# A hybrid encoder layer: the first group's feature-major products computed as seven quarter products in their own stage, and token norms multiplied into the rows

## The chip, the cores and the metric

One core of one Trainium2 chip. The metric is device time in microseconds, median of the runs shown. The profile is one further execution on the same kind of core.

## What is computed

One layer of a bidirectional encoder, on two groups of tokens with shared weights: a sample of 1024 rows and a prompt of 256 rows, each of 2048 features. The kernel treats the 1280 rows as two halves of 640 ("first group" and "second group"). Cut to what matters:

```python
hn = rms_norm(x, norm_g)                       # per row: x / rms(x) * g
proj = hn @ w_in                               # 2048 x 4896
xbc, z_ssd, dt_raw, q, k, v, z_att, mq, z_mem = split_cols(proj, IN_SIZES)
xbc = silu(centred_dwconv(xbc, conv_w, conv_b))     # 5 taps along the tokens, 1536 channels
o_ssd = rms_norm((ssd_fwd + ssd_bwd + d_skip * xs) * silu(z_ssd), ssd_norm_g)
o_att = window_attention(rms_norm(q), rms_norm(k), v, sink) * silu(z_att)
mk, mv = split_cols(rms_norm(mem) @ w_mem_kv, (512, 512))   # 256 memory rows for each request
o_mem = softmax(rms_norm(mq) @ rms_norm(mk)) @ mv * silu(z_mem)
y = x + concat([o_ssd, o_att, o_mem]) @ w_out
```

## The kernel before

**Precision.** Every large product is made of three matmuls of split numbers: an operand is rounded to a high part H, and the rest is a low part L; the products HH, HL and LH are added up in PSUM. `wsplit` (L213) makes the split of a weight tile: a copy on ScalarE (ACT, L215) and a subtraction on VectorE (DVE, L216). The activations are split once for each group into eight tiles `xH0..3`, `xL0..3` (16 feature tiles of 128 by 640 rows) by `fill_direct` (L197): load, then ACT with the gain of the feature, then DVE. The norm of a row is not in there: `x_stats` (L1181) computes 1/rms of each row, tile by tile, and the evictions multiply it in.

**Blocks.** The work of TensorE (PE) is a sequence of blocks, written out at L1316 to L1402. `block_tok` (L239) gives row-major results: for 16 feature tiles k, five row tiles, three matmuls of 512 columns each, 240 in all (192 with the four tiles of the memory rows; 288 columns in the block "kv"). Weights come as tiles of 256 KB from the SP queue, four buffers `wraw`, three each for `wh` and `wl`. `block_feat` (L273) gives feature-major results for 256 output features: 16 k, two halves of features, two halves of rows (320 columns), three matmuls: 192. The convolution's six blocks ("x") and the gates of attention ("za") and memory ("zm"), two each, are made this way, because their results are used with features on partitions; `ev_conv` (L349) multiplies by the norms (`rbc`, a row vector of norms on all partitions, built by the matmuls `prx` in `x_rows`, L1229) and applies the five taps on DVE; `ev_gateT` (L318) makes the gate.

**Order.** mk and mv (memory keys and values), then for the first group q, kv, za, x, mq, zm, z0, z1, for the second kv, x, q, za, z0, z1, mq, zm, then the output: four blocks for the first group, and for the second group eight units of `block_pair` (L1147). That is a 2 x 2 block product by seven quarter products in place of eight (a Strassen scheme): for each unit of two times 128 output features, eight k, seven products, three matmuls of 320 columns: 168. `weight_sums` (L1132) makes the sums of weight quarters on GpSimd (POOL), `seven_sums` and the functions after it (L1052) the sums of row quarters, ahead of time; evictions (`ev_pair`, L1097) add the seven products up.

**Lanes.** All else (statistics, preparation of keys, attention, the scan) is cut into small steps, in two queues called lanes. After each k of a block `pump` (L171) takes steps by the rate in `RATES` or `MR` (steps for each k of lane 0 and lane 1). `need` (L182) runs a lane until something is done. A scheduler places the instructions within each engine's in-order stream: weight splits are drawn ahead by a priority offset, and a lane's instruction is placed no earlier than the last split (`marks`). The lanes' tiles lie in the pools `cl` and `mp`, `w2` (L398) being a ring of five buffers. Statistics pieces (512 features of 128 rows, 256 KB) are loaded by SP into that ring and squared with a sum on ACT (L1187 and L1199). SP issues all loads and stores in order.

The first group's lanes begin with `mem_stats` in the second half of mk; `x_stats` of the first group follow in mv and q.

Of the kernel before, what the change touches and what calls it, by code (L numbers as in the profile page):

```python
# [19 lines left out]
P = 128  # L20
# [6 lines left out]
MR = ((1.0, 0), (1.25, 0))  # L27
# [15 lines left out]
def hymba_encoder_kernel(  # L43
# [3 lines left out]
    mq_norm_g, mk_norm_g, x_turned, mem_turned, w_in_laid, w_mem_laid, w_out_laid, w_out_pairs, vecs,  # L47
# [20 lines left out]
    beside = ExitStack()  # L68
    cl = beside.enter_context(tc.tile_pool(name="cl", bufs=1))
    mp = beside.enter_context(tc.tile_pool(name="mp", bufs=2))  # L70
# [10 lines left out]
    def psum(name):  # L81
# [8 lines left out]
    upper = lconst([P, P], "upper")  # L90
    G.affine_select(out=upper, in_=ones, compare_op=ALU.is_ge, fill=0.0, base=0,
                    pattern=[[1, P]], channel_multiplier=-1)
# [8 lines left out]
    kT = lconst([P, 2, 7 * P], "kT", F32R)  # L101
    kL = lconst([P, 2, 7 * P], "kL", F32R)
    v_all = lconst([P, 7, P], "v_all")
    dt_all = lconst([P, NT, 32], "dt_all")
    eacs_all = lconst([P, NT, 32], "eacs_all")
    cd_all = lconst([P, NT, 32], "cd_all")

    wj_all = lconst([P, 6, 32], "wj_all")
    dd_all = lconst([P, 6, 32], "dd_all")
    rx = const([P, 14], "rx")  # L110
    rxh = const([P, NT], "rxh")
    rbc = lconst([P, 640], "rbc")
    carry = lconst([P, 12, 4], "carry")
    state = lconst([P, 1024], "state")
    mkH = lconst([P, 4, 256], "mkH", F32R)
    mkL = lconst([P, 4, 256], "mkL", F32R)
    mv = lconst([P, 2, 512], "mv")

# [14 lines left out]
    mv_d = dram([P, 2, 512], "mv_d")  # L133
# [63 lines left out]
    def fill_direct(q, j, src, gain=None, n=640):  # L197

        ch = rp.tile([P, 640], F32, tag="ch", name="chd", bufs=CH)[:, :n]
        last_load[0] = S.dma_start(ch, src)  # L200
        yield
        if j == 0:
            new_quad(q)
        h, l = cur["H", q][:, j, :n], cur["L", q][:, j, :n]
        if gain is None:
            A.activation(h, ch, AF.Copy)
            V.tensor_sub(l, ch, h.bitcast(F32))
        else:
            A.activation(h, ch, AF.Copy, scale=gain)
            V.scalar_tensor_tensor(out=l, in0=ch, scalar=gain, in1=h.bitcast(F32), op0=ALU.mult, op1=ALU.subtract)  # L210
        yield
# [98 lines left out]
    def ev_gate(c, base):  # L310
        def f(i, ps):
            z = ev.tile([P, 512], F32, tag="evt" if i % 2 else "evu", name="zs")
            A.activation(z, ps, AF.Tanh, scale=rxh[:, base + i:base + i + 1])
# [4 lines left out]
    def ev_gateT(c, grp, f0):  # L318
        def f(fc, ps):
            th = ev.tile([P, 640], F32, tag="evt", name="th")  # L320
            z = ev.tile([P, 640], F32, tag="evu", name="zs")
            for b in range(2):
                s_ = slice(b * 320, b * 320 + 320)
                V.tensor_mul(z[:, s_], ps[b][:, :320], rbc[:, s_])
            A.activation(th, z, AF.Tanh, scale=0.5)
            V.scalar_tensor_tensor(out=z, in0=th, scalar=1.0, in1=z, op0=ALU.add, op1=ALU.mult)
# [10 lines left out]
    def ev_dtkv(base):  # L337
        def f(i, ps):
            t = base + i
            rt = rx[:, t:t + 1]  # L340
            r = ev.tile([P, P], F32, tag="evt" if i % 2 else "evu", name="kraw")
            A.activation(r, ps[:, 32:160], AF.Copy, scale=rt)
            S.dma_start(k_d[t], r)
            V.scalar_tensor_tensor(out=dt_all[:, t, :], in0=ps[:, :32], scalar=rt, in1=dtb, op0=ALU.mult, op1=ALU.add)
            V.tensor_scalar(out=v_all[:, i + (2 if base else 0), :], in0=ps[:, 160:288], scalar1=rt, scalar2=None,
                            op0=ALU.mult)
        return f

    def ev_conv(grp, f0):  # L349
        def f(fc, ps):  # L350
            fc = f0 + fc
            u = ev.tile([P, 650], F32, tag="evu", name="u")
            if grp == 0:
                n = 638
                V.memset(u[:, :2], 0.0)
                V.tensor_mul(u[:, 2:322], ps[0][:, :320], rbc[:, :320])
                V.tensor_mul(u[:, 322:642], ps[1][:, :320], rbc[:, 320:])
                V.tensor_copy(carry[:, fc, :], u[:, 638:642])
            else:
                n = 646  # L360
                V.tensor_copy(u[:, 0:4], carry[:, fc, :])
                V.memset(u[:, 388:392], 0.0)
                V.memset(u[:, 648:650], 0.0)
                V.tensor_mul(u[:, 4:324], ps[0][:, :320], rbc[:, :320])
                V.tensor_mul(u[:, 324:388], ps[1][:, :64], rbc[:, 320:384])
                V.tensor_mul(u[:, 392:648], ps[1][:, 64:320], rbc[:, 384:])
            cw = [vec[:, R_CW + k * 12 + fc:R_CW + k * 12 + fc + 1] for k in range(5)]
            c = ev.tile([P, 650], F32, tag="evt", name="c")
            V.tensor_scalar(out=c[:, :n], in0=u[:, :n], scalar1=cw[0], scalar2=vec[:, R_CB + fc:R_CB + fc + 1],
                            op0=ALU.mult, op1=ALU.add)  # L370
            for k in range(1, 5):
                V.scalar_tensor_tensor(out=c[:, :n], in0=u[:, k:k + n], scalar=cw[k], in1=c[:, :n],  # L372
                                       op0=ALU.mult, op1=ALU.add)
            th = ev.tile([P, 650], F32, tag="evt", name="tc")
            A.activation(th[:, :n], c[:, :n], AF.Tanh)
            V.scalar_tensor_tensor(out=th[:, :n], in0=th[:, :n], scalar=1.0, in1=c[:, :n],
# [3 lines left out]
            else:  # L380
                S.dma_start(xbc_d[fc, :, 638:1024], th[:, :386])
                S.dma_start(xbc_d[fc, :, 1024:1280], th[:, 390:646])
        return f
# [17 lines left out]
    def ev_mk(i, ps):  # L401
        kr = ev.tile([P, 512], F32, tag="evt" if i % 2 else "evu", name="mkr")
        A.activation(kr, ps, AF.Copy)
        S.dma_start(mq_d[i], kr)

    def ev_mv(i, ps):
        if i < 2:
            A.activation(mv[:, i, :], ps, AF.Copy, scale=rx[:, 10 + i:11 + i])
        else:
            o = ev.tile([P, 512], F32, tag="evu", name="mvo")  # L410
            A.activation(o, ps, AF.Copy, scale=rx[:, 10 + i:11 + i])
            S.dma_start(mv_d[:, i - 2, :], o)

    def mk_prep(i):
        kr = w2("mkr")
        S.dma_start(kr, mq_d[i])
# [26 lines left out]

    def mem_swap(_):

        S.dma_start(mv, mv_d)
# [116 lines left out]
    def attn(t):  # L563
# [12 lines left out]
        A.activation(sq, q, AF.Square, scale=rx[:, t:t + 1])  # L576
# [7 lines left out]
        V.scalar_tensor_tensor(out=q3, in0=q3, scalar=rx[:, t:t + 1], in1=hb(r, 8, 64), op0=ALU.mult, op1=ALU.mult)  # L584
# [99 lines left out]
    def mem_attn(t):  # L684
# [6 lines left out]
        A.activation(sq, q, AF.Square, scale=rx[:, t:t + 1])  # L691
# [6 lines left out]
        V.scalar_tensor_tensor(out=q3, in0=q3, scalar=rx[:, t:t + 1], in1=hb(r, 4, P), op0=ALU.mult, op1=ALU.mult)  # L698
# [81 lines left out]
    def ssd_up(t):  # L780
        first = t in (0, NS)
        last = t in (NS - 1, NT - 1)
        tok = slice(t * P, (t + 1) * P)
        bc = mp.tile([P, 4, P], F32, tag="bc", name="bc", bufs=1)
# [191 lines left out]
    def ssd_down(t):  # L976
# [25 lines left out]
        for g in range(2):  # L1002
# [9 lines left out]
            A.activation(z, y, AF.Square, scale=rxh[:, t:t + 1], accum_out=ss[:, g:g + 1])  # L1012
# [116 lines left out]

    ahead = []  # L1130

    def weight_sums(i):  # L1132

        if i == 64:
            return
# [336 lines left out]
```

## Time and profile before

| what | value |
|---|---|
| median of 3 runs | 1842.91 us (1841.83 to 1843.0) |
| the profiled execution | 1841.09 us, its span 1839.4 us |
| PE, weight loads, DVE, ACT, POOL busy | 1828.2, 1647.2, 1161.1, 825.1, 230.4 us |
| moved by DMA | 289.51 MB, mean 157 GB/s |
| first matmul of mv, q, z1, output units | 49.65, 93.17, 626.43, 1638.27 us |

The span runs from the program's first to its last instruction; the execution's own time has some 2 us around it. Busy time of PE is a union of overlapping matmuls, so 99% does not say that matmuls start at their fastest pace; for that their starts are read in the timeline. A group line has count, busy time, mean length of one, and the idle time before them with what ended it. A DMA line has the size and the median time from issue to landing.

### The profile page before, as it was taken

What the parts mean: (1) busy time and instruction counts of PE and PEld (TensorE: products, weight loads), DVE (VectorE), ACT (ScalarE), POOL (GpSimd) and SP (SyncE); (2) the same over time, 40 slices, a digit from 0 to 9 for tenths busy, and PEclk for the clock granted to TensorE, in tenths of its full rate; (3) what the DMA queues carried; (4) which work ended last, traced back from release to release, by engine and by line L of the source; (5) the groups of instructions that cost most, each with busy time, mean ns of one, the idle gap of its engine ahead of it and who ended that gap; (6) DMA issues with size and microseconds to landing.
All of it is one profiled execution on the core that took longest, in us unless ns stands there. A gap on an engine that the chain in (4) does not pass through costs nothing.

```text
span 1839.4 us, 29987 instructions
## 1 busy us (share of the span) xinstructions
PE 1828.2 (99%) x10786; PEld 1647.2 (90%) x10786; DVE 1161.1 (63%) x2316; ACT 825.1 (45%) x1865; POOL 230.4 (13%) x404
## 2 busy tenths in 40 slices
PE   9999999999999999999999999999999999999999
PEld 8889999998898889999988988887888888889999
DVE  5424555857457466677786666756786554767665
ACT  6553333433534546334345555544565443543332
POOL 0011001000000000001000000001000000048774
PEclk9999999999999999999999999999999999999999
DMA  8763354342442465534445444547686554744442
GB/s 298 252 220 122 113 158 143 110 150 91 138 128 86 149 191 151 147 99 127 130 121 165 158 146 148 159 132 223 212 257 185 174 166 146 237 151 149 144 133 86
DMA packets 198455, 289.51 MB, mean 157 GB/s; under 512 B 18913, under 2 KB 80417, under 8 KB 198305
## 3 DMA queue, kind: packets, MB, share of 16 engines
q1 hardware_dynamic: 198160, 287.53, 50.2%
q8 instruction: 85, 1.39, 0.3%
q14 instruction: 66, 0.53, 0.1%
q10 hardware_dynamic: 144, 0.06, 0.0%
HBM read 230.59 MB, written 56.92 MB: 156 GB/s over the span
## 4 chain that ended last, share of the span: by engine, by line
PE 58%; DVE 2%; DMA 1%; ACT 1%; issue 0%; POOL 0%; DVEq 0%; ACTq 0%; SPq 0%
PE acc L263 8%; PE acc L265 8%; PE acc L264 8%; PE acc L298 5%; PE acc L300 5%; PE acc L299 5%; PE acc L1173 3%; PE acc L1174 3%; PE acc L1172 3%; PE py L909 2%; PE accm L1174 1%; PE accm L1173 1%; PE accm L1172 1%; PE pmo L756 1%; PE po L654 1%; PE pyf L855 1%
## 5 line engine op out<-in xcount | busy, mean ns | idle before, releaser
L216 DVE TENSOR_TENSOR wl<-wraw,wh 128x512 fp32r<-128x512 f32 (+2 forms) x480 | 324.5, 676 | 372.0 <-ACT wh L215 361.4
L215 ACT ACTIVATE wh<-wraw 128x512 fp32r<-128x512 f32 (+2 forms) x480 | 287.1, 600 | 513.8 <-PE acc L265 190.2
L263 PE MATMUL acc<-wh,xH 128*128 128x512 f32 (+1 forms) x1248 | 481.6, 387 | 0.1
L265 PE MATMUL acc<-wh,xL 128*128 128x512 f32 (+1 forms) x1248 | 473.0, 379 | 0.0
L264 PE MATMUL acc<-wl,xH 128*128 128x512 f32 (+1 forms) x1248 | 472.2, 378 | 0.5 <-DVE wl L216 0.5
L298 PE MATMUL acc<-xH,wh 128*128 128x320 f32 x1280 | 401.1, 313 | 0.0
L299 PE MATMUL acc<-xL,wh 128*128 128x320 f32 x1280 | 396.2, 309 | 0.0
L300 PE MATMUL acc<-xH,wl 128*128 128x320 f32 x1280 | 395.9, 309 | 0.0
L263 PEld LDWEIGHTS acc<-wh,xH 128*128 128x128 f32 x1248 | 235.0, 188 | 44.8 <-issue 4.4
L265 PEld LDWEIGHTS acc<-wh,xL 128*128 128x128 f32 x1248 | 234.6, 188 | 43.7 <-issue 0.2
L264 PEld LDWEIGHTS acc<-wl,xH 128*128 128x128 f32 x1248 | 235.1, 188 | 43.0 <-issue 2.3
L298 PEld LDWEIGHTS acc<-xH,wh 128*128 128x128 f32 x1280 | 240.4, 188 | 2.2 <-issue 1.6
L299 PEld LDWEIGHTS acc<-xL,wh 128*128 128x128 f32 x1280 | 240.5, 188 | 1.3 <-issue 1.0
L300 PEld LDWEIGHTS acc<-xH,wl 128*128 128x128 f32 x1280 | 240.3, 188 | 0.2 <-issue 0.2
L215 ACT ACTIVATE sh<-ws 128x512 fp32r<-128x512 f32 x64 | 39.7, 631 | 124.8 <-POOL ws L1144 80.8
L216 DVE TENSOR_TENSOR sl<-ws,sh 128x512 fp32r<-128x512 f32 x64 | 51.5, 806 | 63.5 <-ACT sh L215 62.7
L1144 POOL TENSOR_TENSOR ws<-wraw 128x128 f32<-128x128 f32 x128 | 73.9, 597 | 116.2 <-ACT wh L215 65.4
L372 DVE SCALAR_TENSOR_TENSOR c<-u,vec,c 128x638 f32<-128x638 f32 (+1 forms) x96 | 84.7, 882 | 0.6
L627 ACT ACTIVATE lg<-lg,nm 128x384 f32<-128x384 f32 (+1 forms) x80 | 45.1, 564 | 42.3 <-DVE nm L621 40.6
L892 ACT ACTIVATE rb<-rb,wj_all 128x128 f32<-128x128 f32 x160 | 52.4, 390 | 24.6 <-DMA rb<-ac 24.6
L1173 PE MATMUL acc<-rL,sh 128*128 128x320 f32 x192 | 59.3, 309 | 0.0
L1172 PE MATMUL acc<-rH,sh 128*128 128x320 f32 x192 | 59.3, 309 | 0.0
(330 smaller groups left out, 2605.5 us busy)
## 6 DMA issues: line engine op xcount, KB each, us to landing
wraw<-in_w_in_laid_dram SPq DMA_DIRECT2D x288, 256.0 KB, 2.7
wraw<-in_w_out_laid_dram SPq DMA_DIRECT2D x64, 256.0 KB, 3.1
wraw<-in_w_out_pairs_dram SPq DMA_DIRECT2D x64, 256.0 KB, 2.7
chd<-in_x_turned_dram SPq DMA_DIRECT2D x32, 320.0 KB, 4.8
rf<-ac SPq DMA_DIRECT2D x40, 256.0 KB, 3.6
rb<-ac SPq DMA_DIRECT2D x40, 256.0 KB, 3.9
wraw<-in_w_mem_laid_dram SPq DMA_DIRECT2D x32, 256.0 KB, 4.4
xst<-in_x_sample_dram SPq DMA_DIRECT2D x32, 256.0 KB, 4.4
```

The costliest lines, as they stand in the source:

```text
L215: a = A.activation(h, raw, AF.Copy)
L216: b = V.tensor_sub(l, raw, h.bitcast(F32))
L263: T.matmul(ps[t][:, :n], sh, h[:, :n], start=(k_ == 0), stop=False)
L264: T.matmul(ps[t][:, :n], sh, l[:, :n], start=False, stop=False)
L265: T.matmul(ps[t][:, :n], sl, h[:, :n], start=False, stop=(k_ == KT - 1))
L298: T.matmul(o, sh, cur["H", q][:, m, c], start=(k == 0), stop=False)
L299: T.matmul(o, sh, cur["L", q][:, m, c], start=False, stop=False)
L300: T.matmul(o, sl, cur["H", q][:, m, c], start=False, stop=(k == KT - 1))
L372: V.scalar_tensor_tensor(out=c[:, :n], in0=u[:, k:k + n], scalar=cw[k], in1=c[:, :n], op0=ALU.mult, op1=ALU.add)
L1144: G.tensor_tensor(out=o, in0=x, in1=y, op=op)
L1172: T.matmul(ps[p], h, xh, start=(k_ == 0), stop=False)
L1173: T.matmul(ps[p], h, xl, start=False, stop=False)
```

## The change

- The ten feature blocks of the first group become ten units of seven products, in a stage of its own after q, in the order x0, za0, x1, za1, x2, zm0, x3, zm1, x4, x5. `block_pair` takes the weights, the rows and the eviction as arguments. Sums of row quarters are made during the q block and the first unit (`t_load`, `t_sums`, `t_split`), on POOL for the first six of eight k and on DVE for the last two. Convolution and gate work is left in a queue (`left`) and taken piece by piece, 0.67 pieces after each k (0.87 in the last unit), the rest in kv.
- In a unit all four weight quarters are split from one 512-wide tile (one of them overwritten by a difference), and three sums from one of 384; before it was the other way round.
- The lanes' pools `cl` and `mp` are opened after this stage, in the memory of the stage's own pool `early`. Till then statistics use the eviction buffers (x_stats) and one buffer of `early` (mem_stats). So only statistics run ahead of kv: `x_stats` of the first group in mk and mv, `mem_stats` in q. Keys, attention and the scan of the first group start in or after kv, with higher rates in mq, z0 and z1. For the second group x goes ahead of kv.
- Row norms are multiplied in at the fill, by a DVE pass over each loaded tile, so all statistics of a group have to be done before its fill; the norms vanish from all evictions and from attention and scan. The second group's convolution eviction copies on ACT, and the first tap is on ACT.
- Memory values are stored unscaled, read back and scaled later (`mem_values`).

The core of the diff:

```diff
-MR = ((1.0, 0), (1.25, 0))
+MR = ((2.6, 0), (2.6, 0))
-RATES = ({'q': (1.9, 0), 'kv': (1.3, 0), 'za': (1.2, 0.5), 'x': (1.15, 0.5), 'mq': (1.15, 1.25), 'zm': (1.15, 1.25),
-          'z0': (1.25, 1.25), 'z1': (1.25, 1.25)},
-         {'kv': (1.05, 1.1), 'x': (1.0, 1.15), 'q': (1.35, 2.5), 'za': (1.35, 2.5), 'z0': (1.55, 2.55),
+RATES = ({'q': (1.3, 0), 'kv': (1.3, 1.3), 'mq': (2.2, 1.6), 'z0': (2.2, 1.7), 'z1': (2.2, 1.7)},
+         {'kv': (1.2, 1.4), 'x': (1.75, 1.85), 'q': (1.6, 2.4), 'za': (1.6, 2.4), 'z0': (1.55, 2.55),
...
+        if norm:
+            V.scalar_tensor_tensor(out=ch, in0=ch, scalar=gain, in1=rbc, op0=ALU.mult, op1=ALU.mult)
+            gain = None
...
-            sums = fin.tile([P, 512], F32, tag="ws", name="ws", bufs=3)
+            sums = fin.tile([P, 384], F32, tag="ws", name="ws", bufs=3)
...
+    def t_sums(k):
+        for i, x in enumerate(raw[k]):
+            g_ = R_G + k + 8 * i
+            V.scalar_tensor_tensor(out=x, in0=x, scalar=vec[:, g_:g_ + 1], in1=rbc, op0=ALU.mult, op1=ALU.mult)
+        a, b = [hv(x, 2) for x in raw.pop(k)]
+        t, u = sums[k] = [ev.tile([P, 2, 320], F32, tag=n, name="tt") for n in ("evt", "evu")]
...
+        at = (4, 5, 7, 8, 10, 12, 16, 18)[k]
+        for j, f in ((at - 2, t_load), (at, t_sums), (at + 1, t_split)):
...
-            xt = w2("mst")
+            xt = stat_at[0](c)
...
-    queue(0, mem_stats, range(4))
-    queue(0, vectors, [0])
     queue(0, x_stats, range(5))
-    queue(0, distances, [0])
     queue(0, x_rows, [0])
...
+    stat_at[0] = lambda c: fin.tile([P, 512], F32, tag="xst", name="mst")
+    queue(0, mem_stats, range(4))
+    run(block_tok(w_in_rows("q"), 5, ev_raw(q_d, 0)), RATES[0]["q"], extra=t_step)
+    need(mem_stats, range(4))
+    weight_sums(w_in_pairs, 0)
+    units = [x for i in range(4) for x in ((None, 2 * i), (i // 2, i % 2 * 2))] + [(None, 8), (None, 10)]
+    owe = 0.0
+    for u, unit in enumerate(units):
+        for k in block_pair(w_in_pairs, u, rows_in, ev_seven(*unit)):
+            owe = owe + (0.67 if u < 9 else 0.87) if left else 0.0
+            if owe >= 1:
+                owe -= 1
+                some_left()
+            if u == 0 and k < 7:
+                t_step(16 + k)
+    early.close()
+    cl = beside.enter_context(tc.tile_pool(name="cl", bufs=1))
+    mp = beside.enter_context(tc.tile_pool(name="mp", bufs=2))
```

More of the change, by code (lines that the diff above doesn't have):

```diff
@@ L347, in ev_dtkv @@
-        return f
[L349 to L374, printed above, removed]
@@ L1181, in x_stats, with some_left @@
+    def some_left():
+        with ExitStack() as st:
+            for ins in marks:
+                st.enter_context(tc.issue_after(ins))
+            left.popleft()()
+    stat_at = [lambda c: ev.tile([P, 512], F32, tag="evt" if c % 2 else "evu", name="xst")]
     def x_stats(t):
@@ L1242, in f @@
         def f(q):
+            need(x_rows, [grp])
             return [part(fill_direct, q, j, x_turned[grp, (4 * q + j) * P:(4 * q + j + 1) * P, :],
-                         gain=vec[:, R_G + 4 * q + j:R_G + 4 * q + j + 1]) for j in range(4)]
+                         gain=vec[:, R_G + 4 * q + j:R_G + 4 * q + j + 1], norm=True) for j in range(4)]
         return f
@@ L1343, in hymba_encoder_kernel @@
     queue(0, k_prep, range(5))
+    queue(0, attn, range(4))
     queue(1, dt_prep, [0])
[L1345 to L1349 removed]
     queue(1, ssd_up, range(4))
[L1351 removed]
     tok("mq", w_in_rows("mq"), ev_raw(mq_d, 0))
[L1353 to L1354 removed]
     queue(0, mem_attn, range(5))
     tok("z0", w_in_rows("z0"), ev_gate(0, 0))
[L1357 to L1358 removed]
     tok("z1", w_in_rows("z1"), ev_gate(1, 0), refill_x(1))
+    for b in range(6):
+        feat("x", b, ev_conv(1, 2 * b), 1)
@@ L1363, in hymba_encoder_kernel, with gate @@
     tok("kv", w_kv, ev_dtkv(5), grp=1)
+    def gate(name, c, after=None):
+        for b in range(2):
+            feat(name, b, ev_gateT(c, 1, 2 * b), 1, after if b else None)
     queue(0, k_prep, range(5, 10))
+    queue(0, attn, [4])
     queue(1, dt_prep, [5])
-    queue(0, attn, [4])
-    conv(1)
-    queue(1, ssd_up, range(4, 8))
+    queue(1, ssd_up, range(5, 8))
     tok("q", w_in_rows("q"), ev_raw(q_d, 5), grp=1)
-    gate_att(1)
+    gate("za", 0)
     queue(0, attn, range(5, 10))
```

305 lines of the change are left out of this document (204 added, 101 removed).

## Prediction

> **What bounds the kernel now.** I read the page's busy shares and slices first, then the timeline of TensorE, then the busy time by stage.
>
> ```profile
> span 1839.4 us, 29987 instructions
> PE 1828.2 (99%) x10786; PEld 1647.2 (90%) x10786; DVE 1161.1 (63%) x2316; ACT 825.1 (45%) x1865; POOL 230.4 (13%) x404
> PE   9999999999999999999999999999999999999999
> POOL 0011001000000000001000000001000000048774
> ```
>
> TensorE (PE) is busy 99% of the span. The profiled execution took 1841.1 us, 1.7 us more than its span, and the median of the runs is 1842.9 us. A busy PE may still be waiting inside, as a matmul's 0.31 us overlaps the next one's. So the starts have to be looked at, in the timeline:
>
> ```profile
> 120.37 0.39 PE L263 MATMUL acc<-wh,xH 128*128 128x512 f32 x1
> 120.59 0.39 PE L264 MATMUL acc<-wl,xH 128*128 128x512 f32 x1
> ...
> 299.98 0.31 PE L300 MATMUL acc<-xH,wl 128*128 128x320 f32 x1
> 300.13 0.31 PE L298 MATMUL acc<-xH,wh 128*128 128x320 f32 x1
> 300.28 0.31 PE L299 MATMUL acc<-xL,wh 128*128 128x320 f32 x1
> ```
>
> A matmul of 512 columns starts each 0.227 us and one of 320 each 0.147 us. The busy times by stage (the boundaries are the blocks' first matmuls) show whether that pace holds; columns after the length: PE, PEld, DVE, ACT, POOL busy, granted clock, DMA share, GB/s:
>
> ```profile
> 49.65:93.17 43.52, 43.52 (x194) 36.05 (x192) 21.10 (x33) 26.16 (x50) 2.03 (x4) 1.00 0.77 252
> 93.17:147.57 54.40, 54.40 (x242) 45.06 (x240) 15.79 (x29) 27.68 (x66) 6.38 (x18) 1.00 0.60 199
> 626.43:693.25 66.82, 66.82 (x350) 56.78 (x348) 42.95 (x82) 32.27 (x66) 1.58 (x2) 1.00 0.58 183
> 1367.83:1446.39 78.56, 74.50 (x391) 61.77 (x389) 51.63 (x109) 41.02 (x104) 3.16 (x4) 0.98 0.61 188
> 1638.27:1835.39 197.12, 197.12 (x1344) 197.12 (x1343) 129.16 (x201) 69.20 (x136) 135.94 (x240) 1.00 0.43 135
> ```
>
> The second memory block (first row) needs 192 x 0.227 = 43.5 us and takes 43.5; the q block 240 x 0.227 = 54.4 and takes 54.4; the seven-product stage of the output (last row) 1344 matmuls at 0.1467 us each. The pace is the floor itself. Only the fourth row shows PE idle: 78.56 - 74.50 = 4.1 us. So the time follows the number of matmuls, and whatever waits the change adds come on top uncovered.
>
> **The matmuls: -35.2 us.** Ten feature blocks of the first group issue 10 x 192 = 1920 matmuls of 320 columns; ten units of seven products issue 10 x 8 x 7 x 3 = 1680. In the built order all other matmuls keep their counts. The 240 that go are worth 240 x 0.1467 = 35.2 us; bounds 35.2 to 35.3 (the timeline's 0.147).
>
> **The order moves, at nothing.** Lanes start after the new stage, and kv, mq, z0, z1 take them with higher rates. Their PE work is the same wherever it stands. What it costs is waits, sized below.
>
> **Token norms ahead of the fill: +4 us (0 to 7.5).** `x_stats` of five tiles now runs from the middle of the first memory block, and step 3 of the second waits for it: the `prx` matmuls stand in PE's in-order queue, everything behind them, and the fill waits for their result.
>
> ```profile
> xst<-in_x_sample_dram SPq DMA_DIRECT2D x20, 256.0 KB, 4.9
> mq<-mkr SPq DMA_DIRECT2D x4, 256.0 KB, 3.7
> L1187 ACT ACTIVATE xst<-xst x40: 614/617/633, 93.2 to 407.9; 128x512 f32<-128x512 f32 x40
> DMA to landing us min/median/max: 2.9/4.3/6.2
> L137 POOL TENSOR_TENSOR rx<-rx,mhalf 128x1 f32<-128x1 f32 x14 | 8.7, 622 | 1.2
> ```
>
> The pieces use the four eviction buffers, which the first block's results leave only when stored. With T the end of that block: last copy T+0.6, store 3.7, load 4.3, Square 0.8 with its read-out, reduction and two POOL instructions 1.1: T+10.5. PE is there at T + 36 x 0.227 = T+8.2, so it waits 2.3 us. The fifth tile's last piece reuses a buffer free at T+9.4: T+15.6, where PE comes at 10.5 + 16 x 0.227 = T+14.1: 1.5 us more. With loads of 2.9 us both waits vanish; with 6.2 they make 7.5. I take the median's 4.
>
> **Memory statistics in one buffer: +7 us (0 to 22).** `mem_stats` moves into the q block and has one buffer, where `w2` had five. So each of 16 pieces is load, then Square, then the next load.
>
> ```profile
> mst<-in_mem_sample_dram SPq DMA_DIRECT2D x8, 256.0 KB, 5.1
> L1199 ACT ACTIVATE mst<-mst x16: 614/617/633, 27.7 to 69.9; 128x512 f32<-128x512 f32 x16
> ```
>
> In the built order about one piece stands between two weight splits on ACT, and the 15th stands ahead of the third eviction of q, which the new stage's third product needs. The first Square can run some 4 us ahead of q's start (ACT is two steps ahead), so 14 rounds fit into 54.4 + 4 = 58 us if one takes 4.2 us. A round is landing + 0.62 + about 0.1 us of semaphores. With 5.1 us it is 5.8: 14 x 1.6 = 22 us late. With the 2.9 us of the statistics' fastest load: nothing. The block would ask for weights 4.2 MB, statistics 4.2, rows 6.5 and stores 2, some 17 MB; over 62 us that is 270 GB/s, near the 252 of the second memory block, but it falls as the block stretches. I take 4.0 us of landing: 14 x 0.5 = 7.
>
> If one of these waits passes 3.4 us, a rule comes in. The trace first: around the only long wait of this run the granted clock was below one.
>
> ```profile
> 1360.00:1380.00 20.00, 15.94 (x93) 14.33 (x92) 14.78 (x35) 14.20 (x33) 0.00 (x0) 0.91 0.89 276
> ```
>
> The Trainium skill, "TensorE: Matmul & The Clock Gate", Part 1, says that PE drops to half its clock after an idle window of about 3.4 us and needs a busy one to return. By that rule (the row agrees: 0.91 of 20 us is 1.8 us lost) each such wait would cost 1.7 us more, 3.4 for two; the sum goes without it.
>
> **The new stage itself: +3 us (0 to 35).** TensorE's pace is that of the output's stage, quoted above. DVE has more beside it than there: the conv and gate work of the first group.
>
> ```profile
> L216 DVE TENSOR_TENSOR wl<-wraw,wh 128x512 fp32r<-128x512 f32 x384 | 264.3, 689 | 341.6 <-ACT wh L215 331.3 <-DMA chd<-in_x_turned_dram 4.7 <-DMA wraw<-in_w_in_laid_dram 4.1
> L216 DVE TENSOR_TENSOR sl<-ws,sh 128x512 fp32r<-128x512 f32 x64 | 51.5, 806 | 63.5 <-ACT sh L215 62.7
> L216 DVE TENSOR_TENSOR wl<-wraw,wh 128x384 fp32r<-128x384 f32 x64 | 45.6, 713 | 0.0
> L372 DVE SCALAR_TENSOR_TENSOR c<-u,vec,c 128x638 f32<-128x638 f32 x48 | 42.2, 879 | 0.4
> L376 DVE SCALAR_TENSOR_TENSOR tc<-tc,c 128x638 f32<-128x638 f32 x12 | 9.8, 819 | 1.3 <-ACT tc L375 1.2
> L326 DVE SCALAR_TENSOR_TENSOR zs<-th,zs 128x640 f32<-128x640 f32 x16 | 13.2, 823 | 5.7 <-ACT th L325 5.7
> L1105 DVE TENSOR_TENSOR yr<-acc,yr 128x320 f32<-128x320 f32 x24 | 11.7, 488 | 4.2 <-ACT yu L1109 3.1
> L1105 DVE TENSOR_TENSOR yr<-accm,yr 128x640 f32<-128x640 f32 x8 | 6.5, 812 | 0.0
> ```
>
> Splits 80 x (0.713 + 0.806) = 121.5 us; evictions 10 x (5 x 0.488 + 0.812) = 32.5; twelve features 12 x (4 x 0.879 + 0.819) = 52.0; eight gates 6.6: 213 us of 1680 x 0.1467 = 246 (86%, against 129 of 197, 66%, in the output's stage). A unit that follows a conv unit has 12.2 + 3.3 + 8.7 = 24.2 us of DVE work in 24.6, the others 17: they fit, with up to three steps of splits ahead, and little to spare. Splits on ACT and sums on POOL are those of the output's stage. The upper bound is the last rival's; I take 3, nearest to the row without loss.
>
> **kv and the lanes: +4 us (0 to 12).** Buffers of the lanes start where the new stage's end, so the first `x_stats` load, eight vector loads and four more statistics wait on SP for the stage's last matmul, with kv's sixth weights behind them, while PE has five prefetched steps of 15 x 0.130 = 9.8 us.
>
> ```profile
> L1198 SPq DMA_DIRECT2D mst<-in_mem_sample_dram x8: 423/432/612, 22.3 to 32.6; - x8
> wraw<-in_w_in_laid_dram SPq DMA_DIRECT2D x16, 144.0 KB, 2.1
> ```
>
> Fourteen issues of 0.43 and a landing of 2.1 are 8.1 us, hidden; but the fifth statistics load reuses a buffer that waits for a load (4.3 us) and its use, which puts the weights some 2 to 4 us after PE. I take 2 (0 to 4). The z1 block is the densest: its 42.95 us of DVE (third stage row) contain splits 16 x 0.689 = 11.0, fills 16 x 0.88 = 14.1 and evictions 3.4; the other 14.5 grow by 3.9/2.5, the new rates over the old, to 22.6, and each fill gains a 0.82 us pass: 64 us of a block of 54.4 + 12.4 x 1.56 = 74. That is 87%; 2 more, between nothing and twice the 4.1 us of the fourth stage row. The evictions' lost norm multiplications save DVE time where PE never waited for it: nothing.
>
> ```profile
> L210 DVE SCALAR_TENSOR_TENSOR xL<-chd,vec,xH 128x640 fp32r<-128x640 f32 x40 | 34.1, 880 | 13.7 <-ACT xH L209 13.2 <-DMA gk<-in_k_norm_g_dram 0.4
> L207 DVE TENSOR_TENSOR xL<-chd,xH 128x640 fp32r<-128x640 f32 x8 | 6.4, 818 | 0.1
> ```
>
> **Sum.** 1841.1 - 35.2 + 4 + 7 + 3 + 4 = 1823.9; the median of before stands 1.8 above its profiled execution, so 1825.7, say 1825.
>
> **Rivals.** (1) *All waits are hidden.* For it: nearly every block of before runs at its floor with similar chains beside it. Against it: the one buffer, whose round must not pass 4.2 us. 1842.9 - 35.2 = 1807.7; 1806 to 1813.
>
> (2) *The chains' upper ends.* 7.5 and 16 to 22 us, with 3 and 4: 1842.9 - 35.2 + 30.5 to 36.5 = 1838 to 1844, nearly no gain. For it: loads of 5.1 us; against it: a stretched block loads DMA less.
>
> (3) *Slower: DVE and POOL shut each other out in the new stage.* One line of the sums shows it:
>
> ```profile
> L1144 POOL TENSOR_TENSOR ws<-wraw x128: 452/464/1046, 1621.8 to 1820.8; 128x128 f32<-128x128 f32 x128
> 1638.46 0.54 DVE L216 TENSOR_TENSOR wl<-wraw,wh 128x384 fp32r<-128x384 f32 x1
> ```
>
> A sum takes 0.46 us alone and up to 1.05; a split of 384 columns 0.54 alone and 0.713 in the mean. If they excluded each other for whole durations, a unit needs 32 x 0.464 + 8 x (0.54 + 0.689) = 24.7 us of its 24.6 already; the output's stage, with one more such pass of 0.85 and one of 0.49 a unit, would need 26.0 and lost nothing. So at most 24.64/26.0 = 95% of a duration can exclude. At that share a unit with the conv's 8.7 us takes (24.7 + 8.7) x 0.95 = 31.7, 7.0 over, in five units: 35 us, and with the others' 15: 1842.9 - 35.2 + 50 = 1858. It begins to cost at 24.64/33.4 = 74% and decides (17 us, with 18 around it) at about 84%. The Trainium skill, "SBUF — State Buffer", Who interferes with whom, says that a DVE instruction with two SBUF inputs and a GpSimd one that reads SBUF lock each other out for the whole instruction; conv taps have two such inputs. By that rule it is the case above; the stretched rows agree in kind, the output's stage without loss does not in full.
>
> **Chances.** Forecast (own range 1813 to 1837) 0.48; rival 1 0.22; rival 2 0.16; rival 3 0.14. The range 1807 to 1846 leaves out part of rival 1 and nearly all of rival 3. A difference of 0.2%, 3.7 us, is about what a measurement tells from none: faster is below 1839.2 (0.48 + 0.22 + 0.06 of rival 2 = 0.76), the same up to 1846.6 (0.08), slower 0.16.
>
> **What would show it.** 240 fewer 320-column matmuls at 0.147 us. PE idle before `prx` and at the end of q, named by DMA of `xst` and `mst`, of some microseconds; ACT's wait for `mst` large. In the new stage PE without idle and POOL's sums near 0.6 us: over 0.75 us a sum (3.0 of a step's 3.08), rival 3. The forecast is wrong if a round of `mst` is far from 4.7 us, or if PE waits for the lanes in z0 and z1.

## The result and the profile after

The changed kernel takes 1853.6 us (median of 4 runs, 1852.2 to 1854.6), the kernel before on the same chip 1842.5 (1841.8 to 1843.0). The ratio is 1.006 with a 95% interval of 1.0043 to 1.0077: about 11 us slower. The profiled execution took 1854.6 us.

The page of the changed kernel, head and slices:

```profile
span 1852.9 us, 30542 instructions
PE 1811.6 (98%) x10546; PEld 1616.8 (87%) x10546; DVE 1268.9 (68%) x2424; ACT 902.3 (49%) x2039; POOL 469.0 (25%) x738
PE   9897999998999999999999999999999999999999
POOL 0026888882110000000000000000100000038775
PEclk9898999999999999999999999999999999999999
```

TensorE has its 240 matmuls fewer, but the second and fourth slice (46 us each) show an 8 and a 7 in PE and eights in its granted clock, where PE's slices of before show nines. POOL's eights are the new stage; its 2 and 6 ahead of them are mostly the row sums in q.

Busy time by stage, the boundaries being the first matmuls of mk, mv, q, the new stage, kv, and the output's units (columns: PE, PEld, DVE, ACT, POOL busy, granted clock, DMA share, GB/s):

```profile
5.37:53.19 47.82, 45.98 (x194) 36.08 (x193) 22.01 (x36) 29.80 (x59) 2.81 (x6) 1.00 0.83 276
53.19:107.25 54.06, 47.89 (x204) 39.27 (x203) 31.16 (x45) 25.71 (x51) 1.48 (x4) 0.91 0.68 210
107.25:183.91 76.66, 63.49 (x242) 48.31 (x241) 45.92 (x57) 32.08 (x67) 41.55 (x46) 0.91 0.64 190
183.91:431.92 248.01, 246.55 (x1681) 245.50 (x1680) 208.35 (x306) 115.01 (x205) 205.21 (x306) 1.00 0.39 113
431.92:472.39 40.47, 34.34 (x246) 33.45 (x245) 22.53 (x54) 24.13 (x63) 6.30 (x14) 0.96 0.75 237
1651.36:1848.93 197.57, 197.34 (x1344) 197.08 (x1343) 128.99 (x202) 75.03 (x136) 140.80 (x240) 1.00 0.45 135
```

A block's **floor** is its matmuls at their pace: 43.5 us for mk and mv, 54.4 for q, 246.3 for the stage (1680 at the 0.1466 to 0.1467 of the output's units), 31.3 for kv (240 at 0.130 to 0.131). The fastest stages below come 0.8 us under that floor, so differences of less than 1 us there say nothing. What is over the floor, against the same block before:

| block | over its floor, after | before | more |
|---|---|---|---|
| mk | 4.3 | 0.7 | 3.5 |
| mv | 10.5 | 0.0 | 10.5 |
| q | 22.2 | 0.0 | 22.3 |
| new stage | 1.7 | - | 1.7 |
| kv | 9.2 | 2.2 | 7.0 |
| output units | 0.5 | 0.1 | 0.4 |
| all blocks between kv and the output units (the remainder) | | | 3.3 |

The sum is 48.7 us; less 35.2 for the matmuls it is the 13.5 by which the spans differ. Three quarters of the 48.7 lie ahead of the new stage, in blocks whose own matmuls the change does not touch. The ten `prx` moved from kv into mv; they are 1.2 us of work there (e2's row of mv below: no idle time, 44.68 us), so waits and slow matmuls are 9.3 of mv's 10.5, and in kv they grew by 8.2.

In q, PE is idle for 76.66 - 63.49 = 13.2 us, and the 63.49 busy ones hold 54.4 us of work. Of these 9.1 us, 6.9 are the lower clock (0.09 of 76.66 us); the rest is mainly the last matmul ahead of each wait, which counts as busy for its whole 0.39 us, not for 0.227. TensorE's timeline at the wait in mv shows both kinds of loss, waiting and slow matmuls:

```profile
61.35 0.83 PE L1353 MATMUL prx<-identr,rx 128*128 128x128 f32 x6
68.36 0.80 PE L1353 MATMUL prx<-identr,rx 128*128 128x128 f32 x2 [6.17 <-POOL rx L119]
68.80 0.77 PE L248 MATMUL acc<-wh,xH 128*128 128x512 f32 x1
69.38 0.63 PE L249 MATMUL acc<-wl,xH 128*128 128x512 f32 x1
69.80 0.63 PE L250 MATMUL acc<-wh,xL 128*128 128x512 f32 x1
...
74.47 0.40 PE L249 MATMUL acc<-wl,xH 128*128 128x512 f32 x1
74.70 0.40 PE L250 MATMUL acc<-wh,xL 128*128 128x512 f32 x1
```

Six `prx` matmuls are done, the next ones wait 6.17 us for the fourth tile's norm, and then matmuls start each 0.43 us, not each 0.227, for 5.7 us. So this wait costs 6.2 us and 2.7 more (13 matmuls x 0.2, with the first).

The waits in q, by what ended them (us in total, times, longest):

```profile
ACT tH L1214 <- POOL tt L1206: 20.6, 11, 5.7
ACT mst L1313 <- DMA mst<-in_mem_sample_dram: 10.9, 6, 3.2
PEld acc L248 <- ACT wh L200: 9.9, 5, 3.2
ACT mst L1313 <- DMA mst<-in_mem_prompt_dram: 5.2, 3, 2.6
PE acc L249 <- DVE wl L201: 4.5, 5, 1.7
```

PE waits for the weight splits (`wh`, `wl`). ScalarE, which makes `wh`, had little work (32.1 of 76.66 us) but stood 20.6 us in its order waiting for GpSimd's row sums (`tt`) and 16.1 for the pieces of `mst`. Which of the two sets the block's length a list of waits can't say: each fills time that the other would fill. That is what the runs are for.

### The profile page after: what moved, and what is told of

It reads as the page before. It is cut to its first block, busy times and chain, and to the rows that moved or that the text cites. A ratio compares the mean times of both kernels' runs of the same rounds, so it can differ in the third digit from the quotient of the medians.

```text
span 1852.9 us, 30542 instructions
## 1 busy us (share of the span) xinstructions
PE 1811.6 (98%) x10546; PEld 1616.8 (87%) x10546; DVE 1268.9 (68%) x2424; ACT 902.3 (49%) x2039; POOL 469.0 (25%) x738
## 4 chain that ended last, share of the span: by engine, by line
PE 83%; DMA 7%; DVE 3%; POOL 2%; ACT 2%; issue 2%; SPq 0%; POOLq 0%; ACTq 0%; DVEq 0%
PE acc L248 11%; PE acc L249 11%; PE acc L250 11%; PE acc L1172 5%; PE acc L1170 5%; PE acc L1171 5%; PE acc L283 5%; PE acc L284 5%; PE acc L285 5%; PE accm L1171 2%; PE accm L1170 2%; PE accm L1172 2%; PE py L907 2%; PE po L649 1%; DMA xst<-in_x_sample_dram 1%
## 5 line engine op out<-in xcount | busy, mean ns | idle before, releaser
L248 PE MATMUL acc<-wh,xH 128*128 128x512 f32 (+1 forms) x1248 | 485.7, 391 | 15.8 <-ACT wh L200 14.8
L201 DVE TENSOR_TENSOR wl<-wraw,wh 128x512 fp32r<-128x512 f32 (+1 forms) x480 | 341.3, 712 | 218.4 <-ACT wh L200 212.0
L200 ACT ACTIVATE wh<-wraw 128x512 fp32r<-128x512 f32 (+1 forms) x480 | 292.9, 614 | 328.6 <-PE acc L250 149.6
L249 PEld LDWEIGHTS acc<-wl,xH 128*128 128x128 f32 x1248 | 237.5, 190 | 52.2 <-DVE wl L201 10.3
L283 PE MATMUL acc<-xH,wh 128*128 128x320 f32 x640 | 203.0, 317 | 0.0
L284 PE MATMUL acc<-xL,wh 128*128 128x320 f32 x640 | 198.1, 310 | 0.0
L285 PE MATMUL acc<-xH,wl 128*128 128x320 f32 x640 | 198.1, 310 | 0.0
L201 DVE TENSOR_TENSOR sl<-ws,sh 128x384 fp32r<-128x384 f32 x144 | 102.2, 714 | 84.9 <-ACT sh L200 82.9
L283 PEld LDWEIGHTS acc<-xH,wh 128*128 128x128 f32 x640 | 120.2, 188 | 3.4 <-issue 3.0
L284 PEld LDWEIGHTS acc<-xL,wh 128*128 128x128 f32 x640 | 120.3, 188 | 1.7 <-issue 1.2
L285 PEld LDWEIGHTS acc<-xH,wl 128*128 128x128 f32 x640 | 120.1, 188 | 0.2
L1142 POOL TENSOR_TENSOR ws<-wraw,ws 128x128 f32<-128x128 f32 x144 | 96.3, 669 | 11.3
L1142 POOL TENSOR_TENSOR wraw<-wraw 128x128 f32<-128x128 f32 x144 | 90.0, 625 | 11.3
```

The costliest lines, as they stand in the source:

```text
L200: a = A.activation(h, raw, AF.Copy)
L201: b = V.tensor_sub(l, raw, h.bitcast(F32))
L248: T.matmul(ps[t][:, :n], sh, h[:, :n], start=(k_ == 0), stop=False)
L249: T.matmul(ps[t][:, :n], sh, l[:, :n], start=False, stop=False)
L283: T.matmul(o, sh, cur["H", q][:, m, c], start=(k == 0), stop=False)
L284: T.matmul(o, sh, cur["L", q][:, m, c], start=False, stop=False)
```

## The experiments

**Theories.** T1: the one buffer of `mem_stats` holds q. T2: the row sums on GpSimd, in their chain of load, scale, four sums and split, hold q. T3: the norm prelude (`x_stats` in the eviction buffers, then `prx`) holds mv, and the low clock after the wait adds to it. T4: the second group's statistics hold kv. All runs are compared with the kernel before, run on the same chip (medians 1841.6 to 1842.9):

| run | median us (range) | ratio to before, 95% | over its floor: mk + mv | q | stage | kv |
|---|---|---|---|---|---|---|
| changed kernel | 1853.6 (1852.2-1854.6) | 1.0060, 1.0043-1.0077 | 14.8 | 22.2 | 1.7 | 9.2 |
| e1: four buffers for `mst` | 1845.3 (1842.9-1847.2) | 1.0016, 1.0007-1.0026 | 11.6 | 16.0 | -0.8 | 10.1 |
| e2: eight buffers for `xst` | 1841.8 (1839.4-1844.7) | 0.9998, 0.9989-1.0008 | 1.8 | 20.4 | 1.5 | 8.8 |
| e3: all row sums on VectorE | 1844.1 (1840.0-1848.0) | 1.0010, 1.0001-1.0020 | 11.6 | 10.3 | 4.8 | 11.3 |
| e4: `mst` in the stage, one step | 1852.9 (1851.0-1853.9) | 1.0057, 1.0042-1.0072 | 10.8 | 15.8 | 9.6 | 8.0 |
| e8: `mst` in the stage, two steps | 1847.2 (1845.3-1850.8) | 1.0034, 1.0022-1.0046 | 11.0 | 16.1 | 3.7 | 9.1 |
| e9: e1 + e2 | 1835.5 (1833.7-1836.2) | 0.9965, 0.9952-0.9978 | 1.6 | 17.4 | -0.8 | 10.6 |
| e6: e1 + e2 + e3 | 1826.4 (1825.3-1828.9) | 0.9920, 0.9905-0.9934 | 1.9 | 7.6 | -0.4 | 9.7 |
| e11: e6, `mst` in the stage | 1825.7 (1823.8-1827.2) | 0.9906, 0.9891-0.9920 | 1.2 | 1.2 | 4.8 | 9.0 |
| e7: e6, second `xst` in the stage | 1824.6 (1822.2-1826.9) | 0.9912, 0.9895-0.9928 | 1.3 | 7.4 | 0.6 | 2.6 |
| e10: e7, three pairs' sums on GpSimd | 1831.9 (1830.4-1833.6) | 0.9937, 0.9920-0.9954 | 2.0 | 12.4 | 4.0 | 3.2 |
| e12: e6 again | 1827.3 (1825.4-1831.3) | 0.9923, 0.9911-0.9936 | 3.1 | 7.5 | -0.4 | 9.9 |
| e13: e7 again | 1824.5 (1822.8-1825.3) | 0.9901, 0.9886-0.9916 | 2.4 | 7.1 | 0.5 | 2.7 |

The blocks' numbers are lengths between first matmuls in each run's profile, less the floors. e3 and e4 run mk as the changed kernel does and show 0.3 to 1.4 over, so some 3 us of its 4.3 belong to that one execution.

**e1: four buffers for the memory pieces.**

```diff
-    stat_at[0] = lambda c: fin.tile([P, 512], F32, tag="xst", name="mst")
+    stat_at[0] = lambda c: fin.tile([P, 512], F32, tag=("tH6", "tL6", "tH7", "tL7")[c], name="mst")
```

> The memory-row pieces of mem_stats go through four buffers (the places of tH6, tL6, tH7, tL7, which are not written before step 17) instead of one. T1, the one-buffer chain (load 2.8 to 5.7 us, Square, next load) holds the q block and its row sums behind it: the q block, 76.66 us long with 22.2 us over its matmul work in the changed kernel, comes down to 4 to 8 us over, and the time to about 1836 to 1840 us. T2, the row sums on GpSimd and their four load buffers hold the q block: it stays 18 to 22 us over, the time 1850 to 1854. T3, the norm prelude ahead of the first row chunk: nothing at the prelude changes (mk and mv stay 14 to 15 us over together).

The q block is 6.3 us shorter, not 14 to 18: T1 as stated falls, as a part it stands. ScalarE's wait for `mst` went from 16.1 to 5.3 us, its wait for GpSimd's sums stayed long:

```profile
104.11:174.51 70.40, 59.21 (x241) 46.95 (x240) 49.40 (x59) 34.11 (x71) 46.49 (x52) 0.95 0.64 209
ACT tH L1214 <- POOL tt L1206: 13.7, 10, 3.2
ACT mst L1313 <- DMA mst<-in_mem_sample_dram: 4.0, 2, 3.4
ACT mst L1313 <- DMA mst<-in_mem_prompt_dram: 1.3, 1, 1.3
```

**e2: eight buffers for the token pieces.**

```diff
-    stat_at = [lambda c: ev.tile([P, 512], F32, tag="evt" if c % 2 else "evu", name="xst")]
+    turns = [0]
+    def stat_early(c):
+        turns[0] += 1
+        return fin.tile([P, 512], F32, tag=f"t{'HL'[turns[0] % 2]}{turns[0] // 2 % 4}", name="xst")
+    stat_at = [stat_early]
```

> The token-row pieces of the first group's x_stats go through eight buffers of the early pool instead of the four that the evictions of mk and mv use as well. T3, the norm prelude (pieces wait for buffers that hold evictions, and the first row chunk waits for the prx matmuls): mk and mv, together 14.8 us over in the changed kernel, come down to 2 to 6 us over, the wait of 6.3 us ahead of prx goes, with it the stretch of half clock behind it, and the time comes to about 1841 to 1846 us. T1 and T2 expect the q block to stay 15 to 22 us over here. If the prelude is bound by the loads themselves (20 pieces of 2.8 to 5.7 us) and not by buffers, the time stays at 1850 to 1854.

T3 holds. mk and mv run at their floors but for the `prx` and what mk had over before, PE has no idle time in mv, and the granted clock is 1.00 in both; q is 1.8 us shorter:

```profile
5.37:49.62 44.25, 44.16 (x195) 36.06 (x193) 22.55 (x37) 34.06 (x73) 3.56 (x8) 1.00 0.94 326
49.62:94.30 44.68, 44.68 (x204) 37.17 (x202) 30.94 (x44) 20.83 (x37) 1.29 (x2) 1.00 0.71 232
```

The loads were not the limit: with free buffers the first memory block moves 326 GB/s in place of 276, and the prelude is over in time.

**e3: all row sums on VectorE.**

```diff
-            if k < 6:
+            if k < 0:
```

> The row sums of all eight row pairs on VectorE, none on GpSimd. T2 (GpSimd's 24 sums of 320 columns at about 0.9 to 1 us in a chain of load, scale, four sums, split hold the q block): the q block comes from 22.2 to 5 to 10 us over, the time to 1838 to 1844. T1 (the one buffer of mem_stats): VectorE's sums change nothing, 18 to 24 us over, 1850 to 1856; VectorE takes some 12 us more in q, of which 30 us are free.

T2 holds too: q is 12 us shorter, and at 10.3 over just misses the 5 to 10 it had promised. The stage here is 4.8 us over; e6, which makes the same sums, has none of that, so it is not the sums' price. Its trace shows one long wait of TensorE in the stage, for the copy (`qs`) of q's last results out of PSUM, and ahead of that copy in ScalarE's order a Square that waits for its memory piece:

```profile
172.79 0.63 ACT L1313 ACTIVATE mst<-mst 128x512 f32<-128x512 f32 x1 [2.57 <-DMA mst<-in_mem_prompt_dram]
174.57 0.42 PE L1170 MATMUL acc<-xH,sh 128*128 128x320 f32 x1 [3.78 <-ACT qs L316]
```

The 3.78 us are most of the 4.8. So the one buffer of `mst` also reaches into the stage, on the path that the prediction named. In the changed kernel the same wait was 0.4 us.

**e4 and e8: the memory pieces out of q, into the stage.** 20 pieces of 410 columns in a buffer of their own; in e4 a piece's Square comes one step (3.5 us) after its load, in e8, shown here, two (in e4 `yield` stands once).

```diff
-    queue(0, mem_stats, range(4))
     run(block_tok(w_in_rows("q"), 5, ev_raw(q_d, 0)), RATES[0]["q"], extra=t_step)
-    need(mem_stats, range(4))
...
+                S.dma_start(xt, row[:, c * 410:c * 410 + n])
+                yield
+                yield
+                A.activation(xt, xt, AF.Square, accum_out=s5[:, c:c + 1])
...
             if u == 0 and k < 7:
                 t_step(16 + k)
+            else:
+                with ExitStack() as st:
+                    for ins in marks:
+                        st.enter_context(tc.issue_after(ins))
+                    next(stats, None)
```

> The memory rows' statistics are taken out of the q block and made in the new seven-product stage, in 20 pieces of 410 columns through one buffer of their own, one piece to each step of a unit, so that nothing waits for a piece but its own Square. T1: q comes to 3 to 7 us over, the stage stays within 3 us of its matmul work (ScalarE has 133 of 248 us free there), 1834 to 1840 us. T2: q stays 15 to 20 us over, 1848 to 1853. If pieces in a queue with the weight loads cost the stage something, it shows as more than 4 us over in the stage.

> The changed kernel with the memory rows' statistics in the new stage again, but two steps (7 us) from each piece's load to its Square in place of one. In the run with one step the stage was 9.6 us over, and ScalarE stood 28 us in waits for these loads. If that wait in ScalarE's order was the cause, the stage comes to 1 to 4 us over and the time to 1844 to 1849 us; if it was the added loads beside the weight loads, or the Squares' time on ScalarE, it stays 7 to 10 over and at 1851 to 1854. q stays 14 to 17 over in both.

Without any memory piece q is still 15.8 us over, nearly as with four buffers (16.0): what is left there is T2's. And e4 gives its gain back in the stage, 255.85 us long. The waits of e4 in the stage name the cause, and e8's stage row shows it gone:

```profile
ACT lst L1449 <- DMA lst<-in_mem_prompt_dram: 17.7, 10, 2.9
ACT lst L1449 <- DMA lst<-in_mem_sample_dram: 10.4, 6, 2.6
```

```profile
174.05:424.03 249.98, 246.97 (x1681) 245.52 (x1680) 209.25 (x309) 121.90 (x241) 213.76 (x312) 1.00 0.42 129
```

The Square, waiting 28.1 us in all for its load, stands in ScalarE's order ahead of the weight splits. With a step more between load and Square the same loads and Squares cost 6 us less. Most of the loss was the wait in the order, not the work.

**e9 and e6: what the edits give together.** e9 has the edits of e1 and e2, e6 has e3's as well.

> Four buffers for the memory rows' pieces and eight for the token rows' pieces, with GpSimd's row sums as in the changed kernel: beside the run with all three edits this prices GpSimd's sums by themselves. T2 (the sums are a chain of their own): q 12 to 16 us over, 6 to 10 more than with the sums on VectorE, 1832 to 1837 us. If the sums only lengthened the chain of the memory pieces, q comes to the same as with all three edits, within 2 us, and the stage is nearer to its matmul work.

> The three edits of the first runs at once: four buffers for the memory rows' pieces in q, eight buffers of the early pool for the token rows' pieces, all row sums on VectorE. What each took away alone: 10 us of the prelude (mk and mv 1.8 us over in place of 11 to 15), 6 us and 12 us of the q block's 22. T-sum, the three waits are separate and all of them q's and mv's: q 3 to 8 us over, the time 1823 to 1830 us, faster than the kernel before by 12 to 19. T-one, the edits of q take away the same wait (ScalarE's order, in which both the Square and the split stand ahead of the weight splits): q stays at 10 us over, 1830 to 1834. In both the stage is 2 to 5 us over and kv 9 to 11.

The rows of q, of e9 and then of e6:

```profile
94.05:165.87 71.82, 61.54 (x242) 47.85 (x241) 49.79 (x61) 34.04 (x71) 45.85 (x52) 0.90 0.65 213
```

```profile
94.40:156.42 62.02, 57.11 (x242) 46.41 (x240) 52.14 (x83) 33.77 (x71) 18.99 (x26) 0.94 0.75 247
```

GpSimd's 24 sums cost 9.8 us of q and 9.1 us of the time more than the same sums on VectorE, once both sets of buffers are in. The forecasts met 1826.4 (1823 to 1830) and 1835.5 (1832 to 1837), but e9's q of 17.4 lies above the expected 12 to 16.

**e11 and e10: what is left in q.** e11 is e6 with e8's move; e10 is e7 (below) with the sums of pairs 1, 3 and 5 on GpSimd again.

> The run with three edits, but with the memory rows' statistics in the new stage (20 pieces of 410 columns, two steps from load to Square) in place of the q block. If the memory pieces still hold part of q's 7.6 us (16 Squares of 0.55 us and 16 loads of 256 KB beside the row loads), q comes to 2 to 5 us over, the stage to 2 to 4 over, the time 1824 to 1828 us: a draw. If VectorE alone holds q now, q stays 6 to 8 over, and the stage's share makes it slower, 1827 to 1831 us.

> The run with the second group's statistics in the stage, but the row sums of the pairs 1, 3 and 5 on GpSimd and the other five on VectorE. With all on VectorE the q block was 7.4 us over, VectorE busy 56.7 of 65.7 us there, and its one long wait of TensorE (4 us at 146) ended an unbroken run of VectorE. If VectorE's fullness is what is left in q, moving 12 of 32 sums (0.41 us each, 5 us) away brings q to 3 to 6 us over and the time to 1820 to 1824 us. If GpSimd's chain costs whatever its share, q comes to 9 to 14 us over, 1826 to 1832.

The rows of e11 (q, stage) and of e10 (q):

```profile
93.58:149.19 55.61, 54.70 (x242) 44.97 (x240) 47.37 (x75) 22.92 (x39) 11.09 (x16) 1.00 0.59 176
149.19:400.32 251.13, 247.34 (x1681) 245.53 (x1680) 211.54 (x313) 123.72 (x243) 213.24 (x313) 1.00 0.43 128
```

```profile
94.47:161.32 66.85, 58.47 (x242) 45.76 (x240) 50.95 (x71) 34.02 (x71) 31.36 (x36) 0.95 0.67 216
```

Without memory pieces q is 1.2 us over (less than the 2 to 5 expected), at full clock: the pieces still held 6.4 us of it with four buffers. The stage then pays 5.3 for them (4.8 over, where 2 to 4 were expected), so the time is a draw. VectorE's fullness, which I had suspected, is not what held q: in e11 VectorE makes all sums and is busy 47.4 of 55.6 us, and in e10 taking 12 sums from it makes q 5 us longer. In e10 ScalarE stands 8.0 us waiting for those 12 sums; GpSimd's chain cost even at half the share.

**e7, e12, e13: kv.** e6, with `x_stats` of tiles 5 to 9 made in the stage (25 pieces, two steps each).

```diff
-    queue(1, x_stats, range(5, 10))
+    stats = late([(t, xrow(t)) for t in range(5, 10)])
```

> All three edits, and the second group's x_stats are taken out of kv and its lane and made in the new stage: 25 pieces of 410 columns through one buffer, each with two steps (7 us) from its load to its Square. T4 (the statistics on ScalarE and their loads hold the kv block): kv comes from 9 to 11 us over to 2 to 4, the time 6 to 9 us under the run with three edits, 1816 to 1823 us. If kv is held by the convolutions that are left over and by the loads of the vectors, it stays 7 to 10 us over. The stage should stay within 5 us of its matmul work, since a piece has two steps now: with one step it was 9.6 over.

> The kernel with the three edits once more, beside the next run on one chip, for their difference alone: the first medians were 1826.4 and 1824.6 us, with ranges that overlap, while the stages of the two profiles differ by 6.8 us. Here 1825 to 1829 us.

> The kernel with the three edits and the second group's statistics in the stage once more. T4, kv's statistics are on the path to the end: 5 to 8 us under the run beside it, 1818 to 1823. If what kv gains is lost again in the blocks behind it (mq and z were 8 us longer in its profile), 0 to 3 us under, 1823 to 1827.

T4 holds for the block: kv goes from 9.7 to 2.6 us over, and e7's row of kv shows PE idle for 0.5 us, where the changed kernel's shows 6.1:

```profile
402.44:436.32 33.88, 33.39 (x257) 33.16 (x255) 25.69 (x56) 12.16 (x28) 4.39 (x7) 1.00 0.60 197
```

But the time gained is 1.9 us in the first pair of medians and 2.8 in the second, not the 6 to 9 expected of e7. In the profiles of e13 and e12, kv is 7.2 us shorter, mq, z0 and z1 are 11.4 longer and x and kv of the second group 6.0 shorter: the lanes run ahead, 181 of their matmuls lie between the starts of kv and z1 in place of 126, and after the second kv block the count is 794 in both. A part is a new wait, which e13's timeline of TensorE shows in mq:

```profile
466.90 0.39 PE L250 MATMUL acc<-wh,xL 128*128 128x512 f32 x1
469.54 0.63 PE L419 MATMUL pmk<-identr,mkr 128*128 128x128 f32 x4 [2.25 <-issue]
469.92 0.62 PE L248 MATMUL acc<-wh,xH 128*128 128x512 f32 x1
470.34 0.63 PE L249 MATMUL acc<-wl,xH 128*128 128x512 f32 x1
...
473.65 0.39 PE L248 MATMUL acc<-wh,xH 128*128 128x512 f32 x1
```

The transposes of the key preparation `mk_prep` stand in TensorE's order ahead of the block's next matmuls, and VectorE has their rows ready only at 469.4: 2.25 us of waiting, and 1.7 us more by nine matmuls at 0.43.

The best version (e7, e13) takes 1824.5 us, 0.990 (0.9886 to 0.9916) of the kernel before.

## Why the prediction was wrong

**The matmuls, -35.2: right.** In the new stage PE is busy 246.55 of 248.01 us, in e6 245.75 of 245.85. The pace holds, and the product scheme gives what the count says.

**The stage itself, +3: right (1.7), and rival 3 is refuted.** DVE was busy 208.4 us (213 taken), and GpSimd's weight sums took 0.67 to 0.72 us in the mean in this stage, under the 0.75 named as the mark. The longest of their four groups:

```profile
L1142 POOL TENSOR_TENSOR ws<-wraw,ws 128x128 f32<-128x128 f32 x76 | 54.4, 715 | 6.0
```

These means stand against 0.46 us alone, so the sums are stretched. The Trainium skill, "SBUF — State Buffer", Who interferes with whom, says that a VectorE instruction with two SBUF inputs and a GpSimd one that reads SBUF lock each other out; the stretched rows agree with that in kind, and the stage's length shows that it decided nothing there.

**Memory statistics, +7 (0 to 22): this is the step that failed.** The prediction took the one buffer as all that could hold q, and priced it alone. The row sums, which the change puts beside q, had no term at all; the working priced GpSimd only in the new stage. q lost 22.3. The runs show how that divides (us over the floor of q):

| | memory pieces in one buffer | in four buffers | none in q |
|---|---|---|---|
| row sums on GpSimd | 22.2 (changed kernel) | 16.0 (e1), 17.4 (e9) | 15.8 (e4), 16.1 (e8) |
| row sums on VectorE | 10.3 (e3) | 7.6 (e6) | 1.2 (e11) |

(e9, e6 and e11 have e2's edit as well.) Read down the columns, GpSimd's row sums cost 10 to 15 us. Read along the rows, the memory pieces cost 6 to 9, of which the one buffer is 6.3 beside GpSimd's sums and 2.7 beside VectorE's. The two share time, so their prices depend on which is taken away first, and no single split of the 22.3 is right. The memory term alone came out near its 7, but not as it was priced: a piece landed in 3.4 us in the median where 4.0 was taken, which by the prediction's own sum costs nothing, and beside VectorE's sums 6.4 of the 9.1 stay with four buffers. GpSimd's group in q shows what was there to be sized:

```profile
L1206 POOL TENSOR_TENSOR tt<-ra 128x320 f32<-128x320 f32 x6 | 9.2, 1537 | 58.5 <-DVE ra L1200 54.6 <-DVE rx L1315 3.9
L1206 POOL TENSOR_TENSOR tt<-rb__1150,tt 128x320 f32<-128x320 f32 x2 | 2.8, 1400 | 0.1
L1206 POOL TENSOR_TENSOR tt<-rb__1279,tt 128x320 f32<-128x320 f32 x2 | 1.8, 878 | 0.1
```

The groups' means run from 0.87 to 1.54 us a sum. Each pair has four sums, the third needs the first and the fourth the third, and from the start of the first to the end of the fourth they took 4.3 to 7.1 us. In e6 VectorE makes a sum in 0.48 to 0.61 us, and the four took 2.3 to 5.4:

```profile
L1208 DVE TENSOR_TENSOR tt<-ra 128x320 f32<-128x320 f32 x7 | 3.9, 554 | 0.0
L1208 DVE TENSOR_TENSOR tt<-rb__1429,tt 128x320 f32<-128x320 f32 x2 | 1.2, 608 | 0.0
L1208 DVE TENSOR_TENSOR tt<-rb__1114,tt 128x320 f32<-128x320 f32 x2 | 1.0, 482 | 0.0
```

GpSimd was busy 41.6 of q's 76.7 us (45.8 of the 58.5 us of idle time in the first row are one wait that began ahead of q). So it was not full; what counts is the length of the chain, because the split that needs the sum stands in ScalarE's order ahead of the next weight split. That VectorE's own work is also stretched beside GpSimd's sums (`wl` 760 ns in the mean in q, 702 in e6) can be part of their price; no run separates the two.

**Token norms, +4 (0 to 7.5): the mechanism was right, the size wrong.** In the trace of mv it is 10.5 us: 6.2 of waiting, 2.7 of slow matmuls behind it, 1.2 of the `prx` themselves. e2 takes 11.8 off the time. The chain's rows show where. The columns are start, length, and what:

```profile
49.94 5.08 DMA mr<-mkr
56.72 2.40 DMA xst<-in_x_sample_dram
62.13 4.26 DMA xst<-in_x_sample_dram
68.36 0.80 PE prx L1353 x2
```

The store that frees a buffer took 5.1 us (3.7 taken), and two loads came one after the other behind it, where the prediction had one load ahead of the first four tiles' norms. `prx` stood at 15.2 us after the first block's end (T+10.5 predicted), PE at T+8.2, as worked out. The second wait, for the fifth tile (1.5 us forecast), did not come.

**The clock, left out of the sum: should have been in it.** 2.7 us in mv and 6.9 in q are matmuls at half pace. The Trainium skill, "TensorE: Matmul & The Clock Gate", Part 1, gives an idle window of about 3.4 us as the condition; the wait of 6.17 agrees with it, but e13's wait of 2.25 us was followed by the same half pace. The measurement decides here: a shorter wait can suffice. Several short waits did too: near the end of q three waits of 1.5 to 1.7 us lie between 169 and 175, and behind them the clock was at half:

```profile
175.00:179.00 4.00, 3.89 (x9) 2.78 (x10) 1.62 (x4) 1.72 (x5) 2.00 (x4) 0.50 0.50 128
```

**kv and the lanes, +4 (0 to 12): inside its range, 10.3 in the trace.** kv 7.0 in place of 2, because a Square of `x_stats` in ScalarE's order waits for its load (a median of 5.0 us there, 4.3 taken) ahead of the weight splits; the rest 3.3 in place of 2. The waits of the changed kernel in kv:

```profile
ACT xst L1302 <- DMA xst<-in_x_sample_dram: 8.9, 6, 5.6
PEld acc L248 <- ACT wh L200: 6.4, 2, 5.3
```

**Rivals.** Rival 1 (no wait) is refuted for this order. Rival 2 came nearest in kind: chains at or beyond their upper ends, which with the term it lacked end not at 1844 but at 1854. By the prediction's own sum with the measured terms: 1841.1 - 35.2 + 14.0 (mk and mv) + 22.3 + 1.7 + 10.3 + 0.4 = 1854.6, the profiled time (as it must, since the remainder is in the 10.3). That e6 takes 1826.4, next to the forecast of 1825, is luck: its terms are not the forecast's. Its q is 7.6 us over without the one buffer that the 7 stood for, its stage 0.4 under where 3 over was forecast, and its kv 7.5 more than before where 2 was.

**Open.** Why memory pieces cost the stage 5.3 us in e11 and 2.0 in e8, and the 25 token pieces of e7 1.1; how much of the row sums' price is their chain and how much interference; and what the clock alone costs, which was read from starts of matmuls and not tried.

## What to carry to other kernels

When side work is put beside a block that runs at its floor, list every instruction that stands in an in-order engine's stream ahead of the next thing the bound engine needs, and size for each the whole chain that it waits for, helper engines included; that the helper is idle for nearly half of the block, as GpSimd was in q, says nothing. Where two such chains share a stream, take them away in both orders before a price is put on either. Put a load two steps ahead of its use before anything else in that stream can be held by it. Count the waits of the matmul engine with the half-pace stretch behind them, and look at an added block's neighbours before the block: here the new stage was right to 2 us, and the loss lay ahead of it.

## What the runs showed of the hardware that was not expected

- Matmuls of 512 columns start each 0.43 us in place of 0.227 after a wait: for 5.7 us after a wait of 6.17 us, and for 3.7 us (469.9 to 473.6) after one of 2.25 us. Three waits of 1.5 to 1.7 us within 6 us were followed by a granted clock of 0.50 too.
- A GpSimd sum of 128 x 320 with a busy VectorE beside it took 0.87 to 1.54 us in the means of its groups, on VectorE 0.48 to 0.61.
- The same loads cost 6 us less of TensorE's time with one more step (3.5 us) between load and use (e4, e8).
